# RWKV's triangular inverse formed by doubling on TensorE instead of on VectorE with transfers

## The chip, the cores and the metric

The kernel runs on one core of one Trainium2 chip. The metric is the device time of one execution in microseconds (us). TensorE is called PE here, as in the profile; VectorE is DVE, ScalarE is ACT, GpSimd is POOL, and SP is the engine whose queue issues most of the DMAs.

## The reference

The reference is a model of two layers on 256 tokens of width 1024, in float32. In each layer four mixers (HGRN, GLA, RWKV-7, RetNet) work side by side on columns of one projection `h @ w_in`; an output projection, a residual and a layer norm follow, then a feed-forward part (dense in layer 0, eight experts with top-2 routing in layer 1). The change is in RWKV, whose reference is a scan over tokens:

```python
def step(state, inp):
    rt, wt, kt, vt, kkt, at = inp
    sa = jnp.einsum('bhvk,bhk->bhv', state, -kkt)
    state = (state * wt[:, :, None, :]
             + sa[..., None] * (kkt * at)[:, :, None, :]
             + vt[..., None] * kt[:, :, None, :])
    return state, jnp.einsum('bhvk,bhk->bhv', state, rt)
```

The kernel computes this scan in four chunks of 64 tokens for each of four heads. Within a chunk, token i depends on all earlier tokens j of the chunk through a strictly triangular matrix of 64 by 64. What the scan over tokens does one by one becomes a product with the inverse of the identity minus that matrix; there are 16 such inverses in a layer (four chunks, four heads).

## The kernel before

All weights are float32. A background projection ("fill" below) loads a block of weights to `raw`, ACT rounds it to `wH`, DVE forms the remainder `wL`, and PE multiplies three times for each of eight row blocks: `wH` by the upper half of the activations, `wH` by the lower half, `wL` by the upper. These are the rows `Pws_ps` and `Pas_ps`, matmuls with 256 columns; 48 of them make one projection of 256 columns.

A layer's mixers run in this order (function `mixers`): the projections of RetNet, HGRN and GLA are queued as jobs; then `rwkv` runs, and then RetNet, HGRN and GLA. While RWKV runs, `self.step()` advances the queued jobs by one row block, and `between(n)` advances them by n row blocks and holds the next matmuls of RWKV behind them. What is not advanced by the end of RWKV is advanced when RetNet, HGRN or GLA ask for their columns. A scheduler then fixes the order on each engine; each engine works strictly in its order.

RWKV first computes its columns: `col(3)`, `col(1)`, `col(0)` ahead of the triangular matrices, `col(2)` (the values v) and `col(4)` (the gate) behind them. The products of the chunks' keys and queries (`Prw_pss`, then `rw_S`) give the 16 triangular matrices, which are copied to `rw_AT`, a tile of 128 partitions (two heads of 64 rows) by eight matrices of 64 columns. The inverse before is formed in two parts:

- **16 by 16 blocks on DVE.** `rw_AT` goes to DRAM (`rw_d`) and comes back as `rw_Z`, 64 partitions with one block of 16 by 16 each (eight small DMAs). `invert16` inverts all blocks by doubling from 2 to 16 with elementwise products and sums over `iv_tmp`. The result goes to DRAM (two DMAs) and comes back into `rw_XY` (eight DMAs), X the transposed and Y the plain inverse.
- **From 16 to 32 and 64 on PE.** For m = 16 and 32, `rw_Ao` is `rw_AT` under a mask; one group of 16 matmuls of 64 by 64 multiplies it with X, DVE adds the identity (`rw_Pn`), and two further groups give the new X (only for m = 16; copied out by ACT) and the new Y (copied out by DVE).

Ahead of the second part stand v2 (with its mix with layer 0's values in layer 1), `rw_UV` (v transposed, `Prw_ps7`), `rw_RVO` (scores times v, `Prw_pss2`), `rw_BKT` (`Prw_bkt`) and the gate and bonus (`Prw_gate`, `Prw_bonus`, `rw_W`). Behind it stands the loop over the four chunks (`Prw_pu`, `Prw_pst`, `Prw_po`, `Prw_pss3`), which ends in `rw_OC`; a head norm over `rw_OC` and a transposition (`Prw_ps14`) give RWKV's part of `YT`. In the profile all tiles `Prw_ps1` to `Prw_ps14` are named `Prw_ps`.

HGRN follows RetNet; in layer 1 its gate needs a softmax over two rows (`hg_b`, `hg_m`) on DVE ahead of `hg_kt`, which PE transposes (`Phg_ps`) before it can form HGRN's scores (`Phs_...`). GLA's scores are `Pgs_...`. The output projection (`bank_acc`, `bank_r`) multiplies `YT` in the order of k given by `OUTK`; the late parts of HGRN and GLA (`y_late`) are transposed within it.

A second program for general inputs is built behind a branch; it isn't run in these measurements.

Of the kernel before, what the change touches and what calls it, by code (L numbers as in the profile page):

```python
# [124 lines left out]
class Build:  # L125
# [792 lines left out]
    def invert16(self, Z, Y, X):  # L918

        ve = self.nc.vector  # L920
        ve.tensor_copy(Y.rearrange("p a b -> p (a b)"), self.c["e16"][0:64])
        yf, zf = (t.rearrange("p a b -> p (a b)") for t in (Y, Z))
        ve.tensor_copy(yf[:, 1:256:34], zf[:, 1:256:34])
        for m in (2, 4, 8):
            n = 16 // (2 * m)
            G = self.t2([64, n * m * m], n="iv_G")
            tmp = self.t2([64, n * m, m, m], n="iv_tmp") if n * m ** 3 <= 512 else None
            gv = G.rearrange("p (n j i) -> p n j i", n=n, j=m)
            tv = tmp.rearrange("p (n j) i k -> p n j i k", n=n)
            for x in range(n):  # L930
                a, b = slice(2 * m * x, 2 * m * x + m), slice(2 * m * x + m, 2 * m * x + 2 * m)

                self.tt(tv[:, x], Z[:, a, b][:, :, None, :].to_broadcast([64, m, m, m]),
                        Y[:, b, b].rearrange("p k i -> p i k")[:, None, :, :].to_broadcast([64, m, m, m]), OP.mult)
            ve.tensor_reduce(out=G, in_=tmp.rearrange("p a i k -> p (a i) k"), axis=AX.X, op=OP.add)
            for x in range(n):
                a, b = slice(2 * m * x, 2 * m * x + m), slice(2 * m * x + m, 2 * m * x + 2 * m)

                self.tt(tv[:, x], Y[:, a, a][:, :, None, :].to_broadcast([64, m, m, m]),
                        gv[:, x].rearrange("p k i -> p i k")[:, None, :, :].to_broadcast([64, m, m, m]), OP.mult)  # L940
            for x in range(n):
                a, b = slice(2 * m * x, 2 * m * x + m), slice(2 * m * x + m, 2 * m * x + 2 * m)
                ve.tensor_reduce(out=Y[:, a, b], in_=tv[:, x], axis=AX.X, op=OP.add)
        ve.tensor_copy(X, Y.rearrange("p a b -> p b a"))

# [24 lines left out]
    def rwkv(self, l, glr):  # L970
# [108 lines left out]
        XY = p.tile([128, 2, 8, 64], F32, name="rw_XY")  # L1079
        gp.memset(XY, 0.0)  # L1080

        Z, YX = p.tile([64, 16, 16], F32, name="rw_Z"), self.t2([64, 2, 16, 16], n="rw_Z")
        d1 = self.dp.tile([128, 512], F32, name="rw_d1")
        d2 = self.dp.tile([8, 2, 8, 256], F32, name="rw_d2")
# [103 lines left out]
        off = c["off"].rearrange("p (l i) -> p l i", i=64)  # L1188
        idb = c["id64"][:, None, :].to_broadcast([128, 8, 64])
        for li, m in enumerate((16, 32)):  # L1190
            Ao = self.t2([128, 8, 64], n="rw_Ao")
            self.tt(Ao, AT, off[:, li, None, :].to_broadcast([128, 8, 64]), OP.mult)
            ps = self.mx("Prw_ps11")
            with self.between(FI):
                for n in range(8):
                    for s in range(2):
                        P = slice(64 * s, 64 * s + 64)
                        self.mm(ps[P, n * 64:(n + 1) * 64], Ao[P, n, :], X[P, n, :], True, True)
            Pn = self.t2([128, 8, 64], n="rw_Pn")
            self.tt(Pn, n8(ps), idb, OP.add)  # L1200
            if m == 16:
                ps = self.mx("Prw_ps12")
                with self.between(FI):
                    for n in range(8):
                        for s in range(2):
                            P = slice(64 * s, 64 * s + 64)
                            self.mm(ps[P, n * 64:(n + 1) * 64], Y[P, n, :], Pn[P, n, :], True, True)
                X = self.t2([128, 8, 64], n="rw_X")
                self.act(X, n8(ps))
            ps = self.mx("Prw_ps13")  # L1210
            with self.between(FI):
                for n in range(8):
                    for s in range(2):
                        P = slice(64 * s, 64 * s + 64)
                        self.mm(ps[P, n * 64:(n + 1) * 64], Pn[P, n, :], Y[P, n, :], True, True)
            Y = self.t2([128, 8, 64], n="rw_Y")
            ve.tensor_copy(Y, n8(ps))
# [442 lines left out]
```

## Time and profile before

| what | value |
| --- | --- |
| median of 3 runs | 1102.84 us (1101.68 to 1105.39) |
| profiled execution | 1104.21 us |
| its span | 1102.7 us |
| mean granted clock of PE | 0.971 |
| PE busy | 1045.3 us (95%) |
| DVE busy | 792.8 us (72%) |
| ACT busy | 617.1 us (56%) |
| POOL busy | 67.5 us (6%) |

The profiled execution took 1.4 us more than the median; what its span leaves out is 1.5 us. The span holds layer 0's mixers up to about 200 us, its output projection and dense feed-forward part up to about 430 us, layer 1's mixers up to about 625 us, and the experts from about 660 us on. A stretch's row gives its length, and for each engine the busy time within it; the granted clock is 1.00 at 2.4 GHz and 0.50 at 1.2 GHz, and a mean in between is a mix of the two. A matmul in float32 shows as two records, one of `fp32r` as one. A row of the timeline merges equal instructions that follow each other; its duration runs to the end of the last one, which overlaps the start of the next row.

### The profile page before, as it was taken

To read this page: it belongs to the slowest core of one execution; us is meant where nothing else is said; L and a number is where in the kernel's file an instruction comes from. 1 tells how busy PE (TensorE), PEld (TensorE's weight loads), DVE (VectorE), ACT (ScalarE), POOL (GpSimd) and SP (SyncE) were. 2 spreads that over 40 slices of the span, in tenths; PEclk is the share of its full clock that TensorE was granted. 3 is DMA by queue.
4 is the path that set the end of the run, shared out by engine and by line. 5 is a ranking of instruction groups with operands and counts; after the bars stand their busy time and mean duration, and the time that the engine had idled before them with its cause. 6 is when DMAs were issued, how large, how long until landed. Compare 5 with 4: busy or idle time off the path is not lost. (4 is left out here: it accounts for less than half of the span.)

```text
span 1102.7 us, 17027 instructions
## 1 busy us (share of the span) xinstructions
PE 1045.3 (95%) x6664; PEld 906.6 (82%) x6664; DVE 792.8 (72%) x1171; ACT 617.1 (56%) x871; POOL 67.5 (6%) x92
## 2 busy tenths in 40 slices
PE   7799989999999999899899899999999999999995
PEld 6788878799999888888787677888888888877883
DVE  4584675565656456685673577998999899989986
ACT  4534264345555343633363435787788778777763
POOL 2000021100000002000102140000000000010001
PEclk9899998999999999999987999999999999999998
DMA  9244244336567363343151194998899889988952
GB/s 302 87 111 126 72 154 155 116 110 188 178 189 254 139 209 124 108 116 123 48 183 49 49 362 135 356 381 297 317 353 359 310 307 362 353 274 314 363 192 79
DMA packets 142161, 228.83 MB, mean 208 GB/s; under 512 B 17604, under 2 KB 89848, under 8 KB 142072
## 3 DMA queue, kind: packets, MB, share of 16 engines
q1 hardware_dynamic: 135104, 219.76, 58.4%
q10 hardware_dynamic: 6968, 7.90, 2.2%
q8 instruction: 54, 0.88, 0.3%
q14 instruction: 35, 0.29, 0.1%
HBM read 224.50 MB, written 3.15 MB: 206 GB/s over the span
## 5 line engine op out<-in xcount | busy, mean ns | idle before, releaser
L136 DVE TENSOR_TENSOR wL<-raw,wH 128x1024 fp32r<-128x1024 f32 (+2 forms) x477 | 501.6, 1065 | 164.6 <-ACT wH L133 157.8
L133 ACT ACTIVATE wH<-raw 128x1024 fp32r<-128x1024 f32 (+2 forms) x481 | 442.1, 927 | 272.5 <-PE Pws_ps L146 94.8
L146 PE MATMUL Pws_ps<-XT,wH 128*128 128x256 f32 (+1 forms) x1248 | 234.1, 288 | 9.1 <-DVE rc_x L143 8.3
L146 PE MATMUL Pms_ps<-wH,e_X 128*128 128x512 f32 (+1 forms) x768 | 226.9, 374 | 0.0
L146 PEld LDWEIGHTS Pws_ps<-XT,wH 128*128 128x128 f32 (+1 forms) x1248 | 196.4, 192 | 13.1 <-DVE rc_x L143 9.3
L146 PE MATMUL Pws_ps<-XT,wL 128*128 128x256 f32 (+1 forms) x624 | 178.3, 286 | 0.1
L146 PEld LDWEIGHTS Pms_ps<-wH,e_X 128*128 128x128 f32 x768 | 142.1, 188 | 20.2
L146 PE MATMUL Pms_ps<-wL,e_X 128*128 128x512 f32 (+1 forms) x384 | 144.1, 375 | 1.7 <-DVE wL L136 1.7
L146 PEld LDWEIGHTS Pws_ps<-XT,wL 128*128 128x128 f32 (+1 forms) x624 | 119.7, 192 | 1.1 <-issue 0.3
L146 PE MATMUL bank_dn<-wH,e_aT 128*128 128x512 f32 x352 | 112.9, 398 | 0.3
L146 PE MATMUL Pas_ps<-wH,XT 128*128 128x256 f32 x448 | 96.1, 302 | 4.6 <-ACT p_v L133 3.2
L146 PEld LDWEIGHTS Pas_ps<-wH,XT 128*128 128x128 f32 x448 | 75.8, 200 | 9.8 <-ACT p_v L133 4.5
L146 PEld LDWEIGHTS Pms_ps<-wL,e_X 128*128 128x128 f32 x384 | 72.2, 188 | 13.4 <-DVE wL L136 2.4
L146 PEld LDWEIGHTS bank_dn<-wH,e_aT 128*128 128x128 f32 x352 | 66.0, 188 | 17.2 <-DVE e_X L136 1.6
L146 PE MATMUL bank_dn<-wL,e_aT 128*128 128x512 f32 x176 | 69.8, 396 | 0.0
L146 PE MATMUL Pas_ps<-wL,XT 128*128 128x256 f32 x224 | 67.5, 302 | 0.6 <-DVE wL L136 0.5
L146 PEld LDWEIGHTS Pas_ps<-wL,XT 128*128 128x128 f32 x224 | 44.7, 200 | 3.9 <-DVE wL L136 2.4
L146 PEld LDWEIGHTS bank_dn<-wL,e_aT 128*128 128x128 f32 x176 | 33.1, 188 | 7.6
L146 PE MATMUL bank_acc<-wH,ffn_a 128*128 128x512 f32 x88 | 33.5, 394 | 0.0
L146 PE MATMUL bank_r<-wH,ffn_a 128*128 128x512 f32 x88 | 33.3, 392 | 0.0
L146 PE MATMUL bank_acc<-wH,YT 128*128 128x512 f32 x64 | 26.3, 446 | 1.2 <-ACT YT L133 1.2
L133 ACT ACT_TABLE_LOAD x19 | 24.4, 1283 | 1.6 <-PEq L1647 1.2
(385 smaller groups left out, 1238.1 us busy)
## 6 DMA issues: line engine op xcount, KB each, us to landing
raw<-in_moe_w_down SPq DMA_DIRECT2D x40, 1024.0 KB
raw<-in_moe_w_gate SPq DMA_DIRECT2D x32, 1024.0 KB
raw<-in_moe_w_up SPq DMA_DIRECT2D x32, 1024.0 KB
raw<-in_w_in SPq DMA_DIRECT2D x29, 1024.0 KB
raw<-in_moe_w_gate SPq DMA_DIRECT2D x16, 768.0 KB
raw<-in_moe_w_up SPq DMA_DIRECT2D x16, 768.0 KB
raw<-in_ffn_w_gate SPq DMA_DIRECT2D x11, 1024.0 KB
raw<-in_ffn_w_up SPq DMA_DIRECT2D x11, 1024.0 KB
```

The source lines that it names most:

```text
L133: return self.nc.scalar.activation(out=out, in_=in_, func=func, **k)
L136: return (eng or self.nc.vector).tensor_tensor(out=out, in0=a, in1=b, op=op)
L146: return self.nc.tensor.matmul(out=out, lhsT=lhsT, rhs=rhs, start=start, stop=stop)
```

## The change

The transfers, `invert16`, `rw_XY`, `rw_Z` and the constant `e16` are gone. The mask constant `off` now holds six levels (m = 1, 2, 4, 8, 16, 32). The inverse is formed wholly by the doubling on PE: level 1 transposes the masked matrix with one group of 16 matmuls and adds the identity on DVE; levels 2 to 16 take three groups each, level 32 two. That is 15 groups of 16 matmuls in a layer, of which five stood there before.

The levels stand behind `col(2)`, the new place of `col(4)`, and the mix of v in layer 1, and ahead of `rw_UV`, `rw_RVO` and `rw_BKT`. Each level advances the queued jobs by one row block, levels 2 to 32 by one more between the first group and `rw_Pn`: 11 row blocks in all. The `between(FR)` around the matmuls of `rw_UV`, `rw_RVO` and `rw_BKT`, 24 row blocks before, are gone.

```diff
-    for m in (16, 32):
+    for m in (1, 2, 4, 8, 16, 32):
         off.append(...)
...
-        nc.sync.dma_start(d1, AT.rearrange("p n i -> p (n i)"))
-        place = [(b, slice(16 * b, 16 * b + 16), 16 * (b % 4)) for b in range(8)]
-        for b, P, o in place:
-            nc.sync.dma_start(Z[8 * b:8 * b + 8], d1[P].rearrange("j (n i) -> n j i", n=8)[:, :, o:o + 16])
         if l == 0:
             self.rotary_tables()
-        self.invert16(Z, YX[:, 1], YX[:, 0])
-        for x in range(2):
-            nc.sync.dma_start(d2[:, x], YX[:, x].rearrange("p j i -> p (j i)"))
-        for b, P, o in place:
-            nc.sync.dma_start(XY[P].rearrange("p x n i -> p (x n) i")[:, :, o:o + 16], d2[b].rearrange("x n (j i) -> j (x n) i", j=16))
...
         v2 = col(2)
+        tail = col(4)
...
+        for li, m in enumerate((1, 2, 4, 8, 16, 32)):
+            self.step()
+            Ao = self.t2([128, 8, 64], n="rw_Ao")
+            self.tt(Ao, AT, off[:, li, None, :].to_broadcast([128, 8, 64]), OP.mult)
+            if m == 1:
+                ps = self.mx("Prw_ps10")
+                for n in range(8):
+                    for s in range(2):
+                        P = slice(64 * s, 64 * s + 64)
+                        self.mm(ps[P, n * 64:(n + 1) * 64], Ao[P, n, :], self.ident[P, P], True, True)
+                X, Y = self.t2([128, 8, 64], n="rw_X"), self.t2([128, 8, 64], n="rw_Y")
+                self.tt(X, n8(ps), idb, OP.add)
+                self.tt(Y, Ao, idb, OP.add)
+                continue
+            ps = self.mx("Prw_ps11")
...
+                        self.mm(ps[P, n * 64:(n + 1) * 64], Ao[P, n, :], X[P, n, :], True, True)
+            self.step()
+            Pn = self.t2([128, 8, 64], n="rw_Pn")
+            self.tt(Pn, n8(ps), idb, OP.add)
+            if m < 32:
+                ps = self.mx("Prw_ps12")
...
+                X = self.t2([128, 8, 64], n="rw_X")
+                self.act(X, n8(ps))
+            ps = self.mx("Prw_ps13")
...
+            Y = self.t2([128, 8, 64], n="rw_Y")
+            ve.tensor_copy(Y, n8(ps))
```

In the orders that follow, line numbers are those of each kernel's own file; the changed one is shorter by 33 lines.

SP's queue in layer 0, before, from the last weight loads ahead of the inverse to the last ones of the mixers:

```order
L230 DMA raw<-in_w_in 128x8x256 x6
L1085 DMA rw_d_586<-rw_AT 128x512
L230 DMA raw<-in_w_in 128x8x256
L1088 DMA rw_Z<-rw_d_586 8x16x16 x8
L230 DMA raw<-in_w_in 128x8x32
L230 DMA raw<-in_w_in 128x8x16
L230 DMA raw<-in_w_in 128x8x256
L1100 DMA vd<-rc_x 128x512
L1093 DMA rw_d_587<-rw_Z 8x8x256 x2
L230 DMA raw<-in_w_in 128x8x256
L1095 DMA rw_XY<-rw_d_587 16x16x16 x8
L230 DMA raw<-in_w_in 128x8x256 x5
```

and the same place now:

```order
L228 DMA raw<-in_w_in 128x8x256 x4
L228 DMA raw<-in_w_in 128x8x32
L228 DMA raw<-in_w_in 128x8x16
L228 DMA raw<-in_w_in 128x8x256 x3
L1055 DMA vd<-rc_x 128x512
L228 DMA raw<-in_w_in 128x8x256 x6
```

The transfers of `rw_AT`, `rw_Z` and `rw_XY` are gone from it, and the small loads for `col(4)` (128x8x32 and 128x8x16) stand ahead of the load of `vd`.

PE in layer 0, before, at the level m = 16:

```order
L146 MATMUL Prw_ps_1072<-rw_XY,rw_Ao 64x64 x16
L146 MATMUL Pas_ps_1179<-wL,XT 128x256
L146 MATMUL Pas_ps_1179<-wH,XT 128x256
L146 MATMUL Pas_ps_1180<-wH,XT 128x256
L146 MATMUL Pas_ps_1180<-wL,XT 128x256
L146 MATMUL Pas_ps_1180<-wH,XT 128x256
L146 MATMUL Pas_ps_1179<-wH,XT 128x256
L146 MATMUL Pas_ps_1179<-wL,XT 128x256
L146 MATMUL Pas_ps_1179<-wH,XT 128x256
L146 MATMUL Prw_ps_1091<-rw_Pn,rw_XY 64x64 x16
L146 MATMUL Prw_ps_1110<-rw_XY,rw_Pn 64x64 x16
```

PE now, at the level m = 8 (the levels m = 2, 4 and 16 have the same groups, with 15, 11 and 8 fill matmuls between the first two groups; 13 fill matmuls stand ahead of each next level):

```order
L144 MATMUL Prw_ps_915<-rw_X,rw_Ao 64x64 x16
L144 MATMUL Pas_ps_1273<-wH,XT 128x256
L144 MATMUL Pas_ps_1273<-wL,XT 128x256
L144 MATMUL Pas_ps_1273<-wH,XT 128x256
L144 MATMUL Pas_ps_1274<-wH,XT 128x256
L144 MATMUL Pas_ps_1274<-wL,XT 128x256
L144 MATMUL Pas_ps_1274<-wH,XT 128x256
L144 MATMUL Pas_ps_1273<-wH,XT 128x256
L144 MATMUL Pas_ps_1273<-wL,XT 128x256
L144 MATMUL Prw_ps_944<-rw_Pn,rw_Y 64x64 x16
L144 MATMUL Prw_ps_963<-rw_Y,rw_Pn 64x64 x16
```

The new levels stand in the same form as the two old ones: one group, fill, two groups.

DVE in layer 1, before, at the end of the loop over chunks (`rw_OC`), with RetNet's head norm (`rt_o`) behind it:

```order
L136 TENSOR_TENSOR rw_OC<-Prw_po_5662,rw_RO 64x128 x2
L598 TENSOR_REDUCE hn_s<-rt_o 128x8
L598 TENSOR_REDUCE hn_s<-rw_OC 128x8
L140 TENSOR_SCALAR hn_s<-hn_s 128x8 x2
L136 TENSOR_TENSOR rt_o<-rt_o,hn_s 128x512
L136 TENSOR_TENSOR rw_OC<-rw_OC,hn_s 128x512
L136 TENSOR_TENSOR wL<-raw,wH 128x768
L603 TENSOR_REDUCE hn_s_5763<-hn_sq 128x8
L603 TENSOR_REDUCE hn_s_5676<-hn_sq 128x8
```

and the same place now:

```order
L134 TENSOR_TENSOR rt_o<-rt_o,hn_rs 128x512
L1211 COPY rw_UV<-Prw_pu_5807 64x128 x2
L141 SCALAR_TENSOR_TENSOR rt_o<-rt_o,p_g 128x512
L134 TENSOR_TENSOR rw_OC<-Prw_po_5830,rw_RO 64x128 x2
L134 TENSOR_TENSOR hg_m<-hg_b_5976,hg_b_5978 128x256
L596 TENSOR_REDUCE hn_s<-rw_OC 128x8
L134 TENSOR_TENSOR hg_b_5976<-hg_b_5976,hg_m 128x256
L138 TENSOR_SCALAR hn_s<-hn_s 128x8
L134 TENSOR_TENSOR YT<-Ppy_ps_5939,YT 128x2x256
L134 TENSOR_TENSOR rw_OC<-rw_OC,hn_s 128x512
L134 TENSOR_TENSOR hg_b_5978<-hg_b_5978,hg_m 128x256
L134 TENSOR_TENSOR wL<-raw,wH 128x768
```

RetNet's head norm has moved ahead of the last `rw_OC`, HGRN's softmax (`hg_m`, `hg_b`) directly behind it. On PE the last chunk's `Prw_po` was followed by 42 fill matmuls, `Prw_ps14`, RetNet's transposition, 117 fill matmuls and then `Phg_ps`; now it is followed by 3 fill matmuls, RetNet's transposition, 20 fill, `Prw_ps14`, 37 fill and then `Phg_ps`.

## Rows read from the trace of the kernel before

**Rows 1.** The page, part 1: busy us (share of span) and instructions of each engine.
```profile
PE 1045.3 (95%) x6664; PEld 906.6 (82%) x6664; DVE 792.8 (72%) x1171; ACT 617.1 (56%) x871; POOL 67.5 (6%) x92
```

**Rows 2.** Stretches in us: busy us of each engine, granted clock, DMA.
```profile
core 0: us, PE busy (x) PEld busy (x) DVE busy (x) ACT busy (x) POOL busy (x), PEclk, DMA share, GB/s
65.00:80.00 15.00, 12.30 (x102) 10.72 (x102) 13.93 (x40) 5.80 (x11) 0.20 (x2) 0.89 0.29 92
...
100.00:110.00 10.00, 10.00 (x188) 9.26 (x189) 6.62 (x12) 2.07 (x3) 0.00 (x0) 1.00 0.15 45
...
155.00:175.00 20.00, 19.83 (x117) 16.73 (x116) 12.63 (x25) 9.24 (x22) 1.87 (x4) 0.83 0.41 156
185.00:195.00 10.00, 8.24 (x43) 6.59 (x41) 5.71 (x12) 5.13 (x11) 0.76 (x1) 0.83 0.34 111
475.00:490.00 15.00, 13.88 (x93) 11.18 (x92) 13.53 (x39) 5.72 (x13) 0.20 (x2) 1.00 0.34 102
...
545.00:560.00 15.00, 10.55 (x90) 10.10 (x89) 9.63 (x21) 9.64 (x17) 3.29 (x2) 0.77 0.33 106
575.00:590.00 15.00, 12.33 (x89) 10.47 (x87) 10.42 (x25) 7.91 (x19) 3.82 (x8) 1.00 0.20 70
590.00:610.00 20.00, 20.00 (x77) 15.64 (x77) 6.87 (x16) 7.16 (x18) 4.21 (x4) 0.57 0.16 55
...
625.00:635.00 10.00, 6.52 (x27) 4.96 (x26) 4.96 (x9) 2.98 (x5) 4.08 (x5) 0.87 0.61 157
```

**Rows 3.** PE in time: start us, us, operation, count, in brackets the idle before.
```profile
103.04 0.28 PE L146 MATMUL Pas_ps<-wL,XT 128*128 128x256 f32 x1
103.16 0.28 PE L146 MATMUL Pas_ps<-wH,XT 128*128 128x256 f32 x1
103.37 1.15 PE L146 MATMUL Prw_ps<-rw_Pn,rw_XY 64*64 64x64 f32 x32
104.35 1.10 PE L146 MATMUL Prw_ps<-rw_XY,rw_Pn 64*64 64x64 f32 x32
105.38 0.39 PE L146 MATMUL Pas_ps<-wH,XT 128*128 128x256 f32 x1
...
106.91 0.28 PE L146 MATMUL Pws_ps<-XT,wH 128*128 128x256 f32 x1
107.12 1.15 PE L146 MATMUL Prw_ps<-rw_X,rw_Ao 64*64 64x64 f32 x32
108.19 0.39 PE L146 MATMUL Pws_ps<-XT,wH 128*128 128x256 f32 x1
```

**Rows 4.** SP's own DMA issues in time, layer 0.
```profile
57.52 4.77 SPq L1088 DMA_DIRECT2D rw_Z<-rw_d  x8
...
82.58 5.68 SPq L1095 DMA_DIRECT2D rw_XY<-rw_d  x8
```

**Rows 5.** VectorE: one step of the inverse's levels, layer 0.
```profile
102.32 0.69 DVE L136 TENSOR_TENSOR rw_Pn<-Prw_ps,c_id 128x512 f32<-128x512 f32 x1 [0.70 <-PE Prw_ps L146]
...
105.50 0.69 DVE L1217 COPY rw_Y<-Prw_ps 128x512 f32<-128x512 f32 x1 [0.48 <-PE Prw_ps L146]
106.10 0.68 DVE L136 TENSOR_TENSOR rw_Ao<-rw_AT,c_off 128x512 f32<-128x512 f32 x1
```

**Rows 6.** VectorE: busy us of all that touches iv_tmp, over both layers.
```profile
sum 86.00, DVE 12.03; mean DVE 6.01
```

**Rows 7.** PE in time: three waits.
```profile
75.75 0.42 PE L146 MATMUL Pas_ps<-wH,XT 128*128 128x256 f32 x1 [1.74 <-ACT p_v L133]
...
551.62 1.65 PE L146 MATMUL Prw_ps<-ident,rw_OC 64*64 64x64 f32 x26 [4.45 <-DVE rw_OC L136]
...
632.19 1.03 PE L149 MATMUL Ppy_ps<-ident,y_late 128*128 128x128 f32 x4 [2.28 <-DVE y_late L136]
```

**Rows 8.** Stretch and length, then DVE busy us (count): last rw_OC addition to hg_kt, layer 1.
```profile
541.56:570.98 29.42, 23.42 (x45) 0.88 0.42 140
```

**Rows 9.** The same stretch, VectorE on wL alone.
```profile
541.56:570.98 29.42, 7.79 (x9) 0.88 0.42 140
```

More of the change, by code (lines that the diff above doesn't have):

```diff
@@ L107, in shape_constants @@
     blocks["before"] = (a < b).astype(np.float32) - 1024.0 * (a == b)
-    e16 = np.eye(16, dtype=np.float32).reshape(1, 256)
-    blocks["e16"] = np.broadcast_to(e16, (128, 256)).copy()
     blocks["slot"] = np.broadcast_to(np.arange(128, dtype=np.float32), (128, 128)).copy()
@@ L455, in const @@
             return t
-        for k in ("rmask", "e16", "id64", "off", "swap", "ret"):
+        for k in ("rmask", "id64", "off", "swap", "ret"):
             c[k] = const(k)
@@ L916, in retnet @@
         self.put_y(o, 6)
[L918 to L944, printed above, removed]
     def rwkv_columns(self, l, ci, glr):
@@ L1078, in rwkv @@
             ve.tensor_copy(AT[P], S[P, s, :, :, 64 * s:64 * s + 64].rearrange("p c a i -> p (c a) i"))
[L1079 to L1084, printed above, removed]
-        nc.sync.dma_start(d1, AT.rearrange("p n i -> p (n i)"))
-        place = [(b, slice(16 * b, 16 * b + 16), 16 * (b % 4)) for b in range(8)]
-        for b, P, o in place:
-            nc.sync.dma_start(Z[8 * b:8 * b + 8], d1[P].rearrange("j (n i) -> n j i", n=8)[:, :, o:o + 16])
         if l == 0:
             self.rotary_tables()
-        self.invert16(Z, YX[:, 1], YX[:, 0])
-        for x in range(2):
-            nc.sync.dma_start(d2[:, x], YX[:, x].rearrange("p j i -> p (j i)"))
-        for b, P, o in place:
-            nc.sync.dma_start(XY[P].rearrange("p x n i -> p (x n) i")[:, :, o:o + 16], d2[b].rearrange("x n (j i) -> j (x n) i", j=16))
-        X, Y = XY[:, 0], XY[:, 1]
         v2 = col(2)
+        tail = col(4)
         if l == 0:
@@ L1124, in rwkv @@
             self.tt(v2, v2, dv, OP.add)
+        off = c["off"].rearrange("p (l i) -> p l i", i=64)
+        idb = c["id64"][:, None, :].to_broadcast([128, 8, 64])
+        X = Y = None
+        for li, m in enumerate((1, 2, 4, 8, 16, 32)):
[13 more added lines that the diff above has]
+            ps = self.mx("Prw_ps11")
+            if True:
+                for n in range(8):
+                    for s in range(2):
+                        P = slice(64 * s, 64 * s + 64)
+                        self.mm(ps[P, n * 64:(n + 1) * 64], Ao[P, n, :], X[P, n, :], True, True)
[4 more added lines that the diff above has]
+                ps = self.mx("Prw_ps12")
+                if True:
+                    for n in range(8):
+                        for s in range(2):
+                            P = slice(64 * s, 64 * s + 64)
+                            self.mm(ps[P, n * 64:(n + 1) * 64], Y[P, n, :], Pn[P, n, :], True, True)
+                X = self.t2([128, 8, 64], n="rw_X")
+                self.act(X, n8(ps))
+            ps = self.mx("Prw_ps13")
+            if True:
+                for n in range(8):
+                    for s in range(2):
+                        P = slice(64 * s, 64 * s + 64)
+                        self.mm(ps[P, n * 64:(n + 1) * 64], Pn[P, n, :], Y[P, n, :], True, True)
+            Y = self.t2([128, 8, 64], n="rw_Y")
+            ve.tensor_copy(Y, n8(ps))
         UV = self.tmp(4, [128, 2, 4, 2, 64], n="rw_UV")
@@ L1128, in rwkv @@
         for ch in range(4):
-            with self.between(FR):
+            if True:
                 for a in range(2):
@@ L1140, in rwkv @@
         for ch in range(4):
-            with self.between(FR):
+            if True:
                 for a in range(2):
@@ L1151, in rwkv @@
         for ch in range(4):
-            with self.between(FR):
+            if True:
                 for a in range(2):
@@ L1163, in rwkv @@
         SG = self.t2([128, 2, T], n="rw_SG")
-        tail = col(4)
         self.act(SG[:, 0, :], lr[:, 1, :], AF.Tanh, scale=0.5)
@@ L1187, in rwkv @@
             self.stt(W1[:, a], W1[:, a], pc["lnx_b"][:, a:a + 1], pg[:, a], OP.add, OP.mult)
[L1188 to L1217, printed above, removed]
         OC = self.t2([128, 4, 2, 64], n="rw_OC")
```

## The prediction

> **What bounds the kernel now.** I read the page's busy times first. PE is busy for 95% of the span, DVE for 72% [rows 1]. A busy PE need not be a full one, so I looked at the stretches next. Where the inverse's two PE levels run (100 to 110 us), PE has no idle time and the granted clock is 1.00; that is 2.4 GHz [rows 2]. A fill matmul there follows the one ahead of it after 0.12 us (103.04 to 103.16) [rows 3]. So in this part of the layer PE is what time is spent on, and whatever is added to it lengthens the kernel, unless it fills a gap elsewhere.
>
> Then I looked for the transfers that the change removes. Eight small reads into `rw_Z` occupy SP's queue for 4.77 us and eight into `rw_XY` for 5.68 us in layer 0 [rows 4]. No row of PE waits for them: RWKV's columns, v, `rw_UV`, `rw_RVO`, `rw_BKT` and the gate stand between the transfers and the first use of `rw_XY`. The round trip is hidden already, and taking it away returns nothing by itself.
>
> Last I looked for what PE loses in the mixers. A bound for the loss of a stretch is its length less PE's busy time, plus its length times the missing share of the clock. It gives, from [rows 2]: 65 to 80 us 2.7 + 1.65 = 4.35; 155 to 175 us 0.2 + 3.4 = 3.6; 185 to 195 us 1.8 + 1.7 = 3.5; 475 to 490 us 1.1; 545 to 560 us 4.45 + 3.45 = 7.9; 575 to 590 us 2.7; 590 to 610 us 8.6, with no idle time but a clock of 0.57; 625 to 635 us 3.5 + 1.3 = 4.8. These are the places where time can be won.
>
> **Added on PE: +21.9 us.** A layer gets ten more groups of 16 matmuls: the transposition of level 1 and three groups each at m = 2, 4 and 8. Their price is in the groups that stand there now. A group alone runs from where the next fill would have begun (106.91 + 0.12 = 107.03) to the next fill at 108.19: 1.16 us. Two groups together run from 103.16 + 0.12 = 103.28 to 105.38: 2.10 us [rows 3]. A layer's ten are four alone (the transposition and the first group of three levels) and three pairs: 4 × 1.16 + 3 × 2.10 = 10.94 us. Two layers: 21.9 us. All of it is on PE's path, and nothing is taken from PE.
>
> Back to back, the second group of the pair follows after 104.35 − 103.37 = 0.98 us [rows 3], so going into a small group and out again costs 0.18 us. The Trainium skill, page TensorEngine Tiling (Array Packing), section Key Properties, says that changing the tiling mode, from the full array to quadrants of 64 by 64, drains TensorE. It speaks against a change that puts groups of quadrants between full matmuls. It has no price; the rows have one, 0.18 us, and it is in the sum. Without it the sum would be 20 × 0.98 = 19.6 us.
>
> **The joints of the levels: nothing, while DVE is free.** A level's first group waits for `rw_Ao`, the pair for `rw_Pn`. Now DVE forms `rw_Pn` in 0.69 us after the first group, and after the pair `rw_Y` and `rw_Ao` in 0.69 and 0.68 us [rows 5]; eight and thirteen fill matmuls cover this without idle time [rows 2, 3]. The new order has 8 to 15 and 13 at the same joints. I cost them at nothing. If a `wL` of 0.95 us got ahead of the step on DVE each time, a joint would be open for about that long; this is a rival below.
>
> **Taken from DVE: −4.0 us.** `invert16`'s work on `iv_tmp` is 12.0 us over both layers [rows 6]. The new levels put 12 more operations of 0.69 us [rows 5] on DVE in a layer, about 8 us against the 6 that go, so DVE's total hardly changes, but the work is spread over some 30 us instead of crowding 12. In the crowded stretches DVE is busy for 13.9 and 13.5 of 15 us, and PE loses up to 4.35 and 1.1 us [rows 2]; one wait there is 1.74 us for ACT to free a bank [rows 7]. I take 4.0 of the 5.5, since the rotary tables stay in layer 0's queue. Ends: 0 and −5.5. The levels stand behind `col(2)` and `col(4)` on every queue; SP only loses entries, and ACT's three more copies a layer stand beside idle time (busy 2.1 of 10 us there).
>
> **Behind the levels: +3 us.** `rw_UV`, `rw_RVO`, `rw_BKT`, the gate and the first chunks now have little fill between them: eight matmuls (0.96 us) behind `Prw_ps7`, where DVE must make two copies, and three behind `Prw_pss2`. RetNet's matmuls are used as fill in the chunk loop. The trace of before shows no wait here because fill covered all; the nearest wait is the 1.74 us of [rows 7]. Ends: none, and two such in each layer, 7.0 us. I take 3, less than half, since something still stands at each place.
>
> **The end of RWKV in layer 1: +3 us.** From the last `rw_OC` addition to `hg_kt`, DVE is busy for 23.4 us of 29.4 [rows 8], nine `wL` taking 7.8 of it [rows 9]. PE waits 4.45 us once in it, at `Prw_ps14` [rows 7]; otherwise 159 fill matmuls cover it. In the new order four of the nine `wL` (0.87 each) stand in the stretch and RetNet's norm (about 3 us) has gone ahead: 23.4 − 4.3 − 3 = 16.1 us of DVE. PE has only 60 fill matmuls (7.2 us), one group (1.2) and a transposition (0.6), 9.0 us together. It waits 16.1 − 9.0 = 7.1 us, 2.7 more than now. If DVE also idles for the 6.0 us that it idles now, 8.7 more. Ends 0 and 8.7; I take 3.
>
> **Late stages: −7.6 us.** 13 row blocks a layer that were advanced in RWKV are left for later. Behind `Prw_ps14` the new order has 38 more fill matmuls in layer 1 and 35 in layer 0, 4 us of work each. Layer 1 lost 2.7 + 8.6 = 11.3 us at 575 to 610 us with almost no fill; layer 0, which had some, lost 3.6 + 3.5 = 7.1 in its like stages. I put layer 1 there: −4.3. The whole output projection of layer 1 now stands behind GLA's scores, which covers the 2.28 us wait for `y_late` [rows 7]: −2.3. For layer 0 I take −1. Ends: 0 and all of 11.3 + 4.8 + 7.1 = 23.2.
>
> **Sum.** 21.9 − 4.0 + 3 + 3 − 7.6 = +16.3 us. The profiled execution took 1104.21 us (span 1102.7 us), 1.4 us above the median; on its own time the sum gives 1120.5 us, on the median 1102.84 + 16.3 = 1119 us. All low ends together give 21.9 − 5.5 − 23.2 = −6.8, 1096 us; all high ends 21.9 + 7.0 + 8.7 = 37.6, 1140 us.
>
> **Rivals.** *The late fill wins it back (not slower).* Place: HGRN and GLA in both layers. If the saved row blocks keep PE fed and the clock at 1.00 there, all 23.2 us come back and no new waits arise: 21.9 − 4.0 − 23.2 = −5.3, 1097.5 us. It decides when more than 17.9 of the 23.2 us come back. For it: 8.6 us of the loss are one long stretch at a low clock. Against it: layer 0 had fill and still lost 7 us, and 8 us of fill for both layers must do all of it. Chance 0.11.
>
> *The joints open.* Eighteen of the 20 joints (five levels, two each, two layers) stay open for one `wL` of 0.95 us: +17, 1136 us. For it: in the new order a `wL` stands ahead of nearly every `rw_Pn`. Against it: it is over while the first group runs. Chance 0.11.
>
> *The clock falls in the levels.* If the granted clock is at half through one layer's levels, some 29 us of PE work take 29 us more: 1148 us. Against it: 1.00 at 100 to 110 us, with five such groups in it [rows 2]. Chance 0.04.
>
> *The small matmuls overlap.* A group's even and odd matmuls read and write different halves of the partitions; if the new ones ran side by side the added work would be half: 1119 − 11 = 1108 us. Against it: 32 records take 0.98 us, 31 ns each, and 64 columns at 2.4 GHz are 27 ns by themselves [rows 3]. Chance 0.02. The Trainium skill's page TensorEngine Tiling (Array Packing), section Key Properties, says that different tiles can execute in parallel; by that rule the case would be the rule, and the trace does not agree.
>
> **How the numbers follow.** The forecast has 0.72, the rivals 0.11, 0.11, 0.04 and 0.02. This kernel's measurement can tell 0.3% (3.3 us) from no change. Faster is most of the first rival and a corner of the forecast: 0.11. Same is the rest of that rival and the forecast's low edge: 0.07. Slower: 0.82. The range 1103 to 1134 us leaves out the first rival and part of the low edge (0.12) and the clock and the wide end of the joints (0.07).
>
> **What would show it.** Right: 480 records of the small groups in a layer instead of 160, PE gapless at clock 1.00 through the levels, a period near 6 us for a level, DVE no longer full at 65 to 80 us, a longer wait at `Prw_ps14` or `Phg_ps` in layer 1, and a higher clock in its HGRN and GLA. Wrong: waits for `rw_Pn` or `rw_Ao` at each level, a group that costs clearly more or less than 1.1 us, or late stages at a clock of 1.00 without waits, which would bring the time near or below 1103 us.

## The result and the profile after

The changed kernel takes 1120.2 us (median of four runs), the kernel before 1102.3 us beside it: a ratio of 1.0147, 95% interval 1.011 to 1.0184, or 12 to 20 us more. The prediction was 1119. Four of the changed kernel's eight executions (1134.1 us among these four, and 1139.3, 1143.0 and 1144.4 us of a later series, at a mean clock of 0.951 to 0.962) took over 1.5% longer than its fastest and are left out of the ratio and of its row in the table below.

The profiled execution took 1116.75 us, 3.5 below its median (that of before was 1.4 above its own); its span is 1114.7 us against 1102.7. The page's part 1 of after answers [rows 1], and the stretches of after answer [rows 2] (columns as there):

```profile
PE 1060.9 (95%) x7304; PEld 920.7 (83%) x7304; DVE 799.2 (72%) x1141; ACT 620.1 (56%) x877; POOL 66.5 (6%) x90
```

```profile
44.19:238.10 193.91, 187.02 (x1718) 161.48 (x1719) 126.39 (x242) 79.85 (x149) 16.82 (x21) 0.97 0.33 106
...
461.62:656.64 195.02, 181.20 (x1667) 157.11 (x1667) 121.41 (x228) 81.85 (x151) 16.59 (x21) 0.95 0.35 112
656.64:1114.70 458.06, 441.56 (x2158) 369.52 (x2158) 405.75 (x447) 324.18 (x368) 19.62 (x10) 0.99 0.84 297
...
65.00:80.00 15.00, 15.00 (x238) 14.18 (x237) 11.61 (x18) 5.57 (x10) 0.00 (x0) 1.00 0.46 143
70.00:105.00 35.00, 34.80 (x636) 32.28 (x634) 20.32 (x32) 12.01 (x19) 0.00 (x0) 1.00 0.29 92
105.00:135.00 30.00, 30.00 (x254) 23.76 (x251) 16.43 (x43) 8.29 (x14) 0.00 (x0) 1.00 0.12 36
...
487.00:525.00 38.00, 37.40 (x665) 34.75 (x664) 24.29 (x37) 11.91 (x22) 0.00 (x0) 1.00 0.29 91
525.00:555.00 30.00, 29.77 (x263) 23.97 (x261) 17.80 (x46) 10.84 (x17) 0.76 (x1) 1.00 0.16 45
```

PE has 640 records more, 20 groups of 32. The first two rows are the mixers with the output projection of each layer. The same pieces of before are these:

```profile
45.70:231.02 185.32, 176.96 (x1399) 153.50 (x1399) 124.71 (x257) 77.94 (x146) 16.93 (x21) 0.96 0.35 110
...
454.60:643.14 188.54, 174.15 (x1346) 149.73 (x1346) 116.78 (x243) 80.34 (x148) 16.16 (x22) 0.92 0.34 106
643.14:1102.70 459.56, 441.57 (x2158) 369.50 (x2158) 405.80 (x447) 324.20 (x368) 19.60 (x10) 0.99 0.84 299
```

Layer 0 is 8.6 us longer, layer 1 6.5 us. What lies ahead of the first and behind the second has the same matmuls and is 1.5 us shorter each. So all of the growth is in the two layers' mixers: 15.1 us. Through the levels (70 to 105 and 487 to 525 us) and behind them (105 to 135 and 525 to 555 us) the clock is 1.00 and PE is idle for 0.2, 0.6, 0.0 and 0.2 us.

In PE's time row of after, one group stands alone and one pair together (columns as in [rows 3]):

```profile
86.45 0.28 PE L144 MATMUL Pas_ps<-wL,XT 128*128 128x256 f32 x1
86.66 1.15 PE L144 MATMUL Prw_ps<-rw_Pn,rw_Y 64*64 64x64 f32 x32
87.64 1.10 PE L144 MATMUL Prw_ps<-rw_Y,rw_Pn 64*64 64x64 f32 x32
88.67 0.51 PE L144 MATMUL Pas_ps<-wH,XT 128*128 128x256 f32 x2
...
96.71 0.28 PE L144 MATMUL Pas_ps<-wH,XT 128*128 128x256 f32 x1
96.92 1.15 PE L144 MATMUL Prw_ps<-rw_X,rw_Ao 64*64 64x64 f32 x32
98.00 0.38 PE L144 MATMUL Pas_ps<-wH,XT 128*128 128x256 f32 x1
```

Alone, with the next fill due 0.12 us behind the last: 98.00 − 96.83 = 1.17 us; the pair: 88.67 − 86.57 = 2.10 us. The prediction had 1.16 and 2.10. Of the eight pairs in the trace seven take 2.10 or 2.11 us and one, at 93.17 us, 2.27.

### The profile page after: what moved, and what is told of

It is laid out like the page before. It is cut to its first block, busy times and chain, and to the rows that moved or that the text cites. A ratio compares the mean times of both kernels' runs of the same rounds, so it can differ in the third digit from the quotient of the medians.

```text
span 1114.7 us, 18225 instructions
## 1 busy us (share of the span) xinstructions
PE 1060.9 (95%) x7304; PEld 920.7 (83%) x7304; DVE 799.2 (72%) x1141; ACT 620.1 (56%) x877; POOL 66.5 (6%) x90
## 5 line engine op out<-in xcount | busy, mean ns | idle before, releaser
L134 DVE TENSOR_TENSOR wL<-raw,wH 128x1024 fp32r<-128x1024 f32 (+3 forms) x477 | 502.8, 1068 | 171.8 <-ACT wH L131 164.7
L131 ACT ACTIVATE wH<-raw 128x1024 fp32r<-128x1024 f32 (+3 forms) x481 | 442.1, 927 | 272.1 <-PE Pws_ps L144 90.6
L144 PE MATMUL Pws_ps<-XT,wH 128*128 128x256 f32 (+1 forms) x1248 | 236.5, 289 | 9.5 <-DVE rc_x L141 8.3
L144 PEld LDWEIGHTS bank_dn<-wH,e_aT 128*128 128x128 f32 x352 | 66.0, 188 | 17.2 <-DVE e_X L134 1.7
L144 PEld LDWEIGHTS Pas_ps<-wH,XT 128*128 128x128 f32 x448 | 73.5, 194 | 4.0 <-ACT p_v L131 0.5
L144 PE MATMUL Pas_ps<-wL,XT 128*128 128x256 f32 x224 | 65.0, 292 | 4.6 <-DVE wL L134 4.6
L134 POOL TENSOR_TENSOR hn_rs<-rs_ve,mhalf 128x8 f32<-128x8 f32 x8 | 14.4, 1805 | 185.5 <-DVE rs_ve L138 185.5
```

Source lines behind the costliest of these rows:

```text
L131: return self.nc.scalar.activation(out=out, in_=in_, func=func, **k)
L134: return (eng or self.nc.vector).tensor_tensor(out=out, in0=a, in1=b, op=op)
L144: return self.nc.tensor.matmul(out=out, lhsT=lhsT, rhs=rhs, start=start, stop=stop)
```

## The experiments

Two numbers beside the time are used throughout. **Span times mean clock** takes the span less what the clock cost; it varies less from run to run than the time does. It comes out a little lower at a low clock: a fill matmul then takes 0.215 us and not twice 0.12, and the lower clock may also hide waits. **The loss of a stretch** is, as in the prediction, its idle time plus its length times the missing share of the clock. Medians are in us, ratios are against the runs of before beside them. Before itself had 31 executions, 1093.8 to 1109.2 us.

| kernel | median | ratio, 95% interval | span × clock | clock |
| --- | --- | --- | --- | --- |
| before | 1102.3 | 1 | 1066 to 1075 | 0.963 to 0.984 |
| after | 1120.2 | 1.0147 (1.011 to 1.0184) | 1090 to 1094 | 0.974 to 0.981 |
| b_plus10 | 1124.0 | 1.019 (1.0138 to 1.0241) | 1092 to 1094 | 0.971 to 0.978 |
| b_skip | 1118.6 | 1.0108 (1.0051 to 1.0165) | 1068 to 1071 | 0.957 to 0.964 |
| a_no248 | 1116.8 | 1.0108 (1.0037 to 1.0179) | 1067 to 1075 | 0.951 to 0.968 |
| b_nofr | 1125.1 | 1.0196 (1.0131 to 1.0261) | 1078 to 1081 | 0.955 to 0.967 |
| a_fr | 1127.3 | 1.0237 (1.0179 to 1.0296) | 1081 to 1087 | 0.955 to 0.966 |
| b_fr1 | 1117.2 | 1.0155 (1.0086 to 1.0224) | 1072 to 1078 | 0.956 to 0.967 |
| b_fr2 | 1131.9 | 1.0268 (1.0205 to 1.0331) | 1075 to 1078 | 0.944 to 0.958 |
| a_late | 1115.0 | 1.0131 (1.0072 to 1.0189) | 1088 to 1092 | 0.976 to 0.981 |
| b_skip_nofr | 1108.7 | 1.0058 (1.0022 to 1.0094) | 1069 to 1075 | 0.962 to 0.976 |
| a_nostep | 1130.6 | 1.0279 (1.0177 to 1.0382) | 1088 to 1093 | 0.955 to 0.972 |

**What ten groups cost.** Before, with groups that nobody reads:

```diff
+        for d in range(10):
+            ps = self.mx("Prw_dum")
+            for n in range(8):
+                for s in range(2):
+                    P = slice(64 * s, 64 * s + 64)
+                    self.mm(ps[P, n * 64:(n + 1) * 64], AT[P, n, :], self.ident[P, P], True, True)
         UV = self.tmp(4, [128, 2, 4, 2, 64], n="rw_UV")
```

> The kernel before with ten more groups of 16 matmuls of 64 by 64 in each layer, back to back ahead of rw_UV; nobody reads what they form, and nothing else is changed. Theory (PE is what time is spent on in this part of the layer, so every added group lengthens the kernel): 20 groups x 0.98 us = 19.6 us to the 21.9 us of the prediction, so 1102.3 + 19.6 to 21.9 = 1122 to 1124 us, with no new wait. Rival (gaps elsewhere absorb the groups): less than 1112 us, with idle time of PE in late stages shrinking by 10 us or more.

Measured: 1124.0 against 1103.4 us, 20.6 more (interval 15 to 27). In layer 0 the ten groups stand in one row of PE:

```profile
57.48 9.55 PE L146 MATMUL Prw_dum<-ident,rw_AT 64*64 64x64 f32 x320
66.96 0.51 PE L146 MATMUL Pws_ps<-XT,wH 128*128 128x256 f32 x2
```

Back to back they take 9.5 us, and the kernel pays all of it. Nothing elsewhere absorbs it; the rival falls.

**What the round trip costs before.**

```diff
-        nc.sync.dma_start(d1, AT.rearrange("p n i -> p (n i)"))
...
-        self.invert16(Z, YX[:, 1], YX[:, 0])
...
-            nc.sync.dma_start(XY[P].rearrange("p x n i -> p (x n) i")[:, :, o:o + 16], d2[b].rearrange("x n (j i) -> j (x n) i", j=16))
```

> The kernel before without the transfers of the inverse and without invert16 (the 16 by 16 blocks are left out of the inverse, so the result is not the reference's; the five groups of the upper levels remain). Theory (the round trip is hidden, only the crowding of VectorE at 65 to 80 and 475 to 490 us goes): 0 to 5.5 us less than before, 1097 to 1102 us. Rival (the round trip is paid somewhere that no wait of PE names, through SP's queue or the weight loads behind it): 10 us or more less, under 1093 us, with the weight loads of the mixers landing earlier.

Measured: 1118.6 us, 15 more, with work left out. Both expectations miss. Span times clock is 1068 to 1071, as before: the round trip was hidden. The clock is what fell, to 0.957 to 0.964. With `rw_XY` ready early, the scheduler orders PE otherwise: behind HGRN's first score matmul, 30 fill matmuls are left in layer 1 instead of 46, and 96 instead of 138 in layer 0. PE then has long rows of narrow matmuls in one piece:

```profile
597.38 6.26 PE L146 MATMUL Phs_p1p<-hg_E 64*128 64x128 f32 x36 [0.31 <-DVE hg_E L136]
603.57 1.54 PE L146 MATMUL Ppo_ps<-p_v,lin_S 128*128 128x64 f32 x6
604.87 0.77 PE L146 MATMUL bank_acc<-wL,YT 128*128 128x512 f32 x1
605.44 3.94 PE L146 MATMUL Ppo_ps<-p_v,lin_S 128*128 128x64 f32 x18
```

The row of 36 starts at a clock of 1.00 and ends at 0.50. Before has such a row at 589 to 603 us, with two fill matmuls in it and a clock of 0.58. In after 25 fill matmuls stand in it, and its clock stays up: the row of 36 is two of 18, at 2.72 us each:

```profile
593.95 2.72 PE L144 MATMUL Phs_p1p<-hg_E 64*128 64x128 f32 x18
...
599.76 2.72 PE L144 MATMUL Phs_p1p<-hg_E 64*128 64x128 f32 x18
```

**What nine groups give back.**

```diff
             self.step()
+            if m in (2, 4, 8):
+                self.step()
+                continue
```

> The changed kernel without the levels m = 2, 4 and 8 (their row blocks are still advanced; the inverse is incomplete, so the result is not the reference's). Nine groups in a layer are left out, three alone and three pairs, 3 x 1.16 + 3 x 2.10 = 9.78 us. Theory (the added groups are the price): 2 x 9.78 = 19.6 us less than after, 1120.2 - 19.6 = 1100.6 us, within 4 us. Rival (the fill that was moved is the price): over 1112 us.

Measured: 1116.8 us, only 3.4 below after, though span times clock fell from 1091.7 to 1071.8 (means), 19.9 us. About 2 of these are the lower clock itself. (An estimate: a_no248 ran some 35 us more at half clock; the product counts half of each of these, and fill at 0.215 us a matmul gets 0.12 / 0.215 = 0.56 of it done.) The price of the groups is thus near the expected one, and the time is not: by the time alone the rival (over 1112 us) would have won. Here too the scheduler moved fill forward (68 behind HGRN's first scores in layer 1, after has 163) and the clock fell to 0.951 to 0.968.

**The place of the fill in the kernel before.** Three kernels leave the row blocks ahead of `rw_UV`, `rw_RVO` and `rw_BKT` for later: all 24, 12, and 16.

```diff
-            with self.between(FR):
+            if True:
```

> The kernel before without the row blocks that are held ahead of rw_UV, rw_RVO and rw_BKT (24 in a layer, left for later); the inverse is formed as before. It shows the move of the fill alone. Theory of the prediction (behind the levels 0 to 7 us lost, late stages 7.6 us won for 13 row blocks, up to twice that for 24): -15 to 0 us, if rw_XY is back in time. Rival (the fill is what hides the round trip of the inverse; PE reaches the levels some 17 us earlier and waits for rw_XY, which lands near 88 us in layer 0): waits for rw_XY of 3 to 10 us in a layer, and 0 to 10 us more than before, 1102 to 1112 us.

In b_fr1 the same three places have one row block instead of two:

```diff
-            with self.between(FR):
+            with self.between(1):
```

> The kernel before with one row block instead of two held ahead of each of the 12 pieces of rw_UV, rw_RVO and rw_BKT (12 in a layer left for later). Behind HGRN's first score matmul there are 145 fill matmuls in layer 1 and 186 in layer 0, instead of 46 and 138. Theory (the part of the change that helps is the late fill, not the new inverse): the inverse's data still comes in time, since taking away all 24 row blocks, 17 us, made a wait of 8 us; the product of span and clock stays at 1070 us, the mean clock rises from 0.971 to about 0.98, and the time is 5 to 11 us below before, 1092 to 1098 us. Rival (late fill is worth nothing in the kernel before, or rw_XY is waited for): 1102 us or more, with a wait for rw_XY of over 2 us in a layer.

In b_fr2 only the last two places change:

```diff
-            with self.between(FR):
+            with self.between(0):
```

> The kernel before with the row blocks ahead of rw_UV kept (8) and those ahead of rw_RVO and rw_BKT left for later (16 in a layer). 127 fill matmuls are left behind HGRN's first score matmul in layer 1 and 195 in layer 0. Theory: 16 row blocks are 11.5 us of 17, so rw_XY is waited for by 0 to 3 us a layer; product of span and clock 1070 to 1076 us, clock near 0.975 to 0.98, 1092 to 1102 us. Rival (fill early or late is all the same): the clock stays at 0.971 and the waits come on top, 1103 to 1109 us.

Measured: 1125.1, 1117.2 and 1131.9 us, all slower than before; all three theories of a gain fall, and b_nofr and b_fr2 lie above their rivals' ranges too. PE in time, from b_nofr and then b_fr1:

```profile
71.47 0.48 PE L146 MATMUL Prw_ps<-ident,rc_x 64*64 64x64 f32 x4 [9.30 <-DVE rc_x L143]
...
487.86 1.03 PE L146 MATMUL Prw_ps<-rc_x,rw_v 128*32 128x256 f32 x2 [8.27 <-issue]
```

```profile
73.79 0.48 PE L146 MATMUL Prw_ps<-ident,rc_x 64*64 64x64 f32 x4 [3.01 <-DVE rc_x L143]
```

The wait is not for `rw_XY` but earlier, for v (in layer 1 the row names no releaser; it is the first matmul that reads v). In b_fr2 it is 6.17 us in layer 0 and 4.53 in layer 1. Its tile `rc_x` stands on DVE among `invert16`'s operations, and while PE waits, DVE is busy nearly throughout (8.86 of 9.20 us); so what PE waits for is DVE's work in its order, and no wait of DVE for the transfer into `rw_Z` shows. First DVE in time, then the stretch of the wait:

```profile
66.30 0.16 DVE L923 COPY rw_Z<-rw_Z 64x8 f32<-64x8 f32 x1
...
70.25 0.68 DVE L935 TENSOR_REDUCE iv_G<-iv_tmp 64x64 f32<-64x512 f32 x1
70.86 0.47 DVE L143 SCALAR_TENSOR_TENSOR rc_x<-Pws_ps,psmall,rc_sh 128x256 f32<-128x256 f32 x1
```

```profile
62.20:71.40 9.20, 0.00 (x0) 0.00 (x0) 8.86 (x32) 2.45 (x4) 0.10 (x1) 0.71 0.70 225
```

So the held row blocks are part of what hides the inverse's work on DVE; the prediction named RWKV's columns and the gate as what stands between the transfers and the use of `rw_XY`, and left out that v itself stands behind `invert16` on DVE. Whether they also keep the clock up is not shown. In b_fr1 the late stage of layer 1 gains (table below), but `rw_RVO`, `rw_BKT` and the gate, now with 5 fill matmuls between rows of 32, run at 0.54:

```profile
506.00:521.00 15.00, 15.00 (x68) 11.63 (x68) 2.09 (x5) 3.42 (x7) 0.00 (x0) 0.54 0.29 93
```

After has five fill matmuls in the same stretch and runs it at 1.00 in both layers. Over the profiles of all kernels, this stretch (from `rw_RVO` to the bonus) has 12 fill matmuls or fewer 17 times: 4 of them ran at 0.56 to 0.60 and 13 at 1.00.

**The place of the fill in the changed kernel.**

```diff
-            if True:
+            with self.between(FR):
```

> The changed kernel with the row blocks back ahead of rw_UV, rw_RVO and rw_BKT (24 in a layer, as before); the levels keep theirs. Behind HGRN's first score matmul this leaves 0 fill matmuls in layer 1 and 64 in layer 0, where the changed kernel has 163 and 210 and the one before 46 and 138. Theory (late fill that breaks up the long rows of narrow matmuls in HGRN and GLA keeps the granted clock up, the term 'late stages'): the product of span and mean clock stays at after's 1091 us within 5, the clock in HGRN and GLA falls as in the kernel before or below, and the time is 8 to 20 us more than after, 1128 to 1140 us. Rival (the fill's place does not matter): 1117 to 1123 us at after's mean clock of 0.974 to 0.981.

Measured: 1127.3 us, a little under the expected 1128. Span times clock was expected within 5 of 1091 and is 1081 to 1087; the early fill may also cover waits. The medians put the late fill at 7 us of time in the changed kernel, the ratios (1.0237 and 1.0147) at 10; their intervals just touch. HGRN, GLA and the output projection of layer 1, in before, after and a_fr:

```profile
572.90:640.80 67.90, 60.90 (x307) 48.80 (x305) 33.40 (x66) 30.94 (x63) 12.12 (x17) 0.85 0.27 89
```

```profile
576.30:654.20 77.90, 71.58 (x426) 60.50 (x424) 42.24 (x75) 37.30 (x74) 12.62 (x17) 0.93 0.44 143
```

```profile
609.60:669.70 60.10, 48.95 (x224) 39.74 (x224) 27.24 (x58) 23.86 (x52) 12.19 (x17) 0.69 0.17 56
```

The losses are 7.0 + 10.2 = 17.2, 6.3 + 5.5 = 11.8 and 11.2 + 18.6 = 29.8 us. A second profile of after (a_again, below) lost 6.3 + 5.4 = 11.7 us there, though its whole took 26 us longer:

```profile
602.50:680.30 77.80, 71.50 (x425) 60.51 (x423) 42.15 (x75) 37.22 (x74) 12.62 (x17) 0.93 0.43 143
```

For the same stage of each kernel's profile, with the fill counted in PE's order:

| fill matmuls behind HGRN's first scores, layer 1 | loss of the stage, us |
| --- | --- |
| after 163, a_again 163, a_late 158, b_fr1 145 | 11.8, 11.7, 9.9, 8.4 |
| a_nostep 140, b_skip_nofr 127, b_fr2 127, b_nofr 102 | 21.1, 20.8, 23.6, 20.5 |
| a_no248 68, before 46, b_plus10 45 | 26.1, 17.2, 19.8 |
| b_skip 30, a_fr 0 | 36.6, 29.8 |

One profile stands behind each number, and the middle rows show no order; but with 145 or more the loss is the smallest, and with 30 or fewer the largest. The fill is not all of it: in the output projection PE waits 2.5 to 5.7 us for `YT` in b_plus10, b_skip, b_skip_nofr, b_nofr, b_fr2, a_nostep and a_no248, and 1.2 us at most in the others.

**The place of the levels.** The six levels go behind `rw_W`, where two stood before:

```diff
-        for li, m in enumerate((1, 2, 4, 8, 16, 32)):
...
         UV = self.tmp(4, [128, 2, 4, 2, 64], n="rw_UV")
...
             self.stt(W1[:, a], W1[:, a], pc["lnx_b"][:, a:a + 1], pg[:, a], OP.add, OP.mult)
+        for li, m in enumerate((1, 2, 4, 8, 16, 32)):
```

> The changed kernel with the six levels put behind rw_W, just ahead of the loop over chunks, where the two levels stood before; nothing is left out. 158 fill matmuls remain behind HGRN's first score matmul in layer 1 and 181 in layer 0, about as in the changed kernel. Theory (the place of the levels is of no weight, their 15 groups are): the product of span and clock stays at 1091 us within 4 and the time within 6 us of after, 1114 to 1126 us. Rival (the place ahead of scores times v is worth something, or costs something): a difference of 8 us or more, with waits at the joints of the levels or behind them.

Measured: 1115.0 us, inside the expected 1114 to 1126; the interval of its ratio overlaps after's. "Ahead of scores times v" has no weight that these runs can measure.

**The steps within the levels.**

```diff
-            self.step()
             Ao = self.t2([128, 8, 64], n="rw_Ao")
...
-            self.step()
             Pn = self.t2([128, 8, 64], n="rw_Pn")
```

> The changed kernel without the 11 row blocks that its levels advance (left for later or placed by the scheduler); nothing else is changed. Theory (the joints are covered by 8 to 15 fill matmuls, and 206 of 263 fill matmuls remain ahead of the chunk loop in layer 0): some joints have less fill than the 0.95 us that VectorE needs, so 0 to 1 us of wait at up to four joints in a layer; product of span and clock 1091 to 1097 us, time within 8 us of after, 1114 to 1128 us. Rival (the joints open): waits for rw_Pn or rw_Ao at most of the ten joints of a layer, 1136 us or more.

Measured: 1130.6 us, 2.6 above the expected range. The joints held: one wait, 0.56 us at `rw_Ao`. Span times clock is 1088 to 1093, as after's. What was missed is the clock again, 0.955 to 0.972.

**The change with its groups for nothing.** b_skip, with the three held places taken out as well:

```diff
-            with self.between(FR):
+            if True:
```

> The kernel before without the transfers of the inverse and without invert16 (the 16 by 16 blocks are left out, so the result is not the reference's), and without the row blocks ahead of rw_UV, rw_RVO and rw_BKT. It is what the change would be if its ten added groups in a layer cost nothing. 127 fill matmuls stand behind HGRN's first score matmul in layer 1 and 219 in layer 0, where the kernel that only leaves out the transfers has 30 and 96. Theory (with no round trip to wait for, late fill raises the clock in HGRN and GLA): no wait of PE at the transpositions for rw_UV, product of span and clock 1068 to 1074 us, late clock losses in layer 1 below 6 us instead of 25.6, and 1090 to 1105 us. Rival (the falls of the clock only move to where the fill was taken from): product the same, but clock 0.965 or lower and over 1108 us.

Measured over ten runs: 1108.7 us, ratio 1.0058 (1.0022 to 1.0094). The wait for v is gone, as the theory had it, but the stage in layer 1 still lost 20.8 us. The time is the rival's (over 1108), and the clock, 0.962 to 0.976, is for the most part above the rival's 0.965: moving the fill gains nothing over before, even without the round trip. Against after, span times clock is 20 us lower on average (1071.5 to 1091.7), which is the groups' price once more; the time is only some 10 us lower by the ratios.

**The changed kernel once more.**

> The changed kernel itself, once more, with a profile of its own: which falls of the granted clock come back at the same place, and which come by chance. Theory (the falls behind idle time of PE, at rc_x, at the end of RWKV and at GLA's scores, belong to the order; those in gapless stretches come and go): the waits of 4 us at rc_x and 1 to 2 us at rw_OC and gs_E return with their falls, the product of span and clock is 1091 within 4, the time 1115 to 1125 us. Rival (all of the clock follows from the order): the same list of falls within 2 us each.

Measured: 1117.6 us once, as expected, and 1139.3 to 1144.4 us three times, with span times clock at 1085 to 1091. The profile is of an execution of 1143.0 us at a clock of 0.951 and serves here only to see which falls of the clock move. The waits return (4.51 at `rc_x`, 1.23 at `rw_OC`, 1.15 at `gs_E`), and with the first and the last of them the falls behind them. Others come and go. First after, then a_again:

```profile
104.00:122.00 18.00, 18.00 (x166) 13.82 (x162) 8.68 (x22) 4.02 (x8) 0.00 (x0) 1.00 0.00 1
128.00:149.00 21.00, 17.62 (x160) 14.92 (x160) 15.86 (x38) 11.86 (x19) 4.25 (x3) 1.00 0.16 51
```

```profile
104.00:122.00 18.00, 18.00 (x160) 14.03 (x159) 9.29 (x21) 3.93 (x8) 0.00 (x0) 1.00 0.00 1
128.00:149.00 21.00, 20.60 (x103) 17.39 (x102) 10.85 (x29) 8.47 (x12) 1.78 (x1) 0.51 0.00 1
```

The same order runs the end of the chunk loop at 1.00 once and at 0.51 the other time, with PE without a gap ahead of it. So the order alone does not decide whether a fall comes there; what does stays open, and two profiles can't say how often.

## Why the prediction was right, and where it was not

- **PE as the bound:** right. Ten idle groups a layer cost 20.6 us of time.
- **Added, +21.9:** right in size. In the trace of after a group alone costs 1.17 us and a pair 2.10, as priced. Nine of the ten groups a layer were priced at 19.6 and took 19.9 of span times clock, some 18 without the lower clock's share; from before to after it rises from about 1071 to 1091.7. A group in a row of ten costs 0.95 us, so going in and out costs some 0.2 us where I had 0.18. The small matmuls do not overlap here: 320 records in 9.5 us are 30 ns each. The Trainium skill, page TensorEngine Tiling (Array Packing), section Key Properties, has a drain at a change of mode, and the 0.2 us fit it. It also says that different tiles can run in parallel; the two quadrants of these groups write one PSUM tile, no overlap shows, and quadrants that write different ones were not tried.
- **Joints, 0:** right; 0.60 us once in layer 1, otherwise under 0.2. So the rival of the open joints did not come, nor did that of a clock that falls within the levels (1.00 in both layers).
- **Taken from DVE, −4.0:** the mechanism was right, the size nearer to its end of −5.5. At 65 to 80 us the loss of 4.35 is gone, DVE busy 11.6 of 15 us instead of 13.9; in layer 1, whose mixers start 7 us later now, the idle time at the same place (459 to 487 us before, 466 to 494 now) fell from 1.1 to 0.1. In b_skip, which leaves out the same work, PE is busy for all of 65 to 80 us too, yet span times clock is only some 1 us lower than before: other waits took the place, such as one of 5.7 us for `YT` in the output projection.
- **Behind the levels, +3:** wrong; 0.0 and 0.2 us of idle time in the rows above. I priced it by a wait for ACT, but RetNet's matmuls (`Prt_ps`) stand among `rw_BKT`, the gate and the chunks as fill, and the copies were done in time.
- **End of RWKV in layer 1, +3:** wrong in sign. From the last `rw_OC` addition to `hg_kt`, the stretch of [rows 8], PE lost 4.6 + 3.5 = 8.1 us before and 4.8 + 1.8 = 6.6 now:

```profile
541.56:570.98 29.42, 24.84 (x198) 23.51 (x199) 23.42 (x45) 17.51 (x29) 3.29 (x2) 0.88 0.42 140
```

```profile
558.05:574.30 16.25, 11.44 (x95) 10.12 (x96) 15.81 (x33) 7.73 (x14) 1.64 (x1) 0.89 0.18 56
```

  I had DVE's work right (16.1 forecast, 15.81 busy), and DVE sets the length. But PE is idle for 4.8 us and not 7.1. The step that failed is the price of PE's 60 fill matmuls: I took all at 0.12 us, and for some 3.6 us of the stretch (twice 1.8) they ran at half clock, 0.215 us each, and so covered some 1.6 of the 2.3 us between 7.1 and 4.8. I also compared waits alone and left the 3.5 us standing that the clock cost before. The waits came at the fill, which waited for `wL` from the busy DVE (3.19 and 1.03 us), and not at `Prw_ps14` or `Phg_ps`, where I had looked for them:

```profile
562.44 0.39 PE L144 MATMUL Pas_ps<-wL,XT 128*128 128x256 f32 x1 [3.19 <-DVE wL L134]
...
564.15 0.41 PE L144 MATMUL Pas_ps<-wL,XT 128*128 128x256 f32 x1
564.36 0.63 PE L144 MATMUL Pas_ps<-wH,XT 128*128 128x256 f32 x2
564.79 0.41 PE L144 MATMUL Pas_ps<-wL,XT 128*128 128x256 f32 x1
...
570.24 0.39 PE L144 MATMUL Pas_ps<-wL,XT 128*128 128x256 f32 x1 [1.03 <-DVE wL L134]
```

- **Late stages, −7.6:** the mechanism was right, the size 2 us too large. Layer 1 gave back 17.2 − 11.8 = 5.4 us of the 6.6 forecast, with the wait for `y_late` down from 2.28 [rows 7] to 0.85 us; layer 0's like stage (loss 7.5 before, 7.6 now) gave nothing of its 1. After's second profile lost 11.7 us there again, and a_fr, with the late fill taken away, 29.8.
- **The sum:** by the rows at the top the losses of the mixers fell from 15.8 to 12.7 us in layer 0 and from 29.5 to 23.6 in layer 1, 9.0 together, where the prediction's other terms had 5.6. The two digits of the clock leave up to 1 us open in each of the four; with the clock unrounded (0.9552 and 0.9185 before, 0.9737 and 0.9502 now, from the traces' clock records) it is 10.9. The length grew by 15.1, so 26 us of work at full clock were added, 4 more than the ten groups' price. The bound makes up about 1 of the 4: at 0.215 us a fill matmul at half clock, a microsecond there loses less than half. The other 3 I could not place; it wasn't tried. +16.3 thus came out near by luck as well: the term of the groups was right, and the misses of the others offset each other.
- **What can be told apart:** I had 0.3%. The 31 executions of before, one order, range over 1.4%, so a term of 1 to 3 us that is read from one profile of each kernel is not proven by it.
- **The rival "late fill wins it back":** fell. Of its 23.2 us, 5.4 came back.

## What to carry to other kernels

Where one engine is busy all the time, work that moves onto it is paid in full, and a round trip that no wait names can give nothing back when it goes, as here. Before moving fill, find what it hides where it is (here a wait for v behind the inverse on DVE, 3 to 9 us), and read the granted clock there before and after. A kernel with work left out is not a bound on the time if a scheduler reorders the rest: compare span times clock beside the time.

## What was not expected of the hardware

The granted clock moved the time nearly as much as the change did. One and the same kernel before ran at 0.984 and 1093.8 us and at 0.963 and 1108.7 us. Falls also came without idle time of PE ahead of them, behind small matmuls with fill between; b_skip in layer 1, the last gapless 12 us and the fall:

```profile
472.00:484.00 12.00, 12.00 (x121) 11.21 (x121) 6.55 (x10) 4.19 (x8) 0.10 (x1) 1.00 0.31 95
484.00:492.00 8.00, 8.00 (x47) 7.37 (x46) 1.65 (x2) 2.73 (x6) 0.00 (x0) 0.57 0.35 106
```

Span times clock falls a little with the clock: in before it was 1075 at 0.984 and 1066 at 0.963. About 3 of these 9 us are what fill at 0.215 instead of 0.24 us makes (an estimate, as for a_no248, for 47 us more at half clock). Hidden waits may be part of the rest, which is not shown.
